# A ninth seven-product pair in a ConvFFN up-projection, next to the step into the down-projection

## The chip, the cores and the metric

The kernel runs on one core of one Trainium2 chip. The metric is the device time of one execution in microseconds, as the median of several runs. The profile is taken from one further execution; its span runs from the first to the last instruction in the trace, and its own device time is given beside it.

## The reference

One layer of a hybrid decoder trunk over 512 tokens of width 1024, all in float32: three causal token mixers whose outputs are gated and merged, then a causal ConvFFN. The change touches only the ConvFFN:

```
def conv_ffn(h, w_up, conv_w, conv_b, w_down):
    up = h @ w_up                      # 512 x 1024 by 1024 x 5632
    padded = jnp.pad(up, ((0, 0), (CONV_WIDTH - 1, 0), (0, 0)))
    conv = conv_b + conv_w[0] * padded[:, 0:T]
    for i in range(1, CONV_WIDTH):
        conv = conv + conv_w[i] * padded[:, i:i + T]
    gate, val = jnp.split(conv, 2, axis=-1)
    return (jax.nn.gelu(gate, approximate=True) * val) @ w_down   # 2816 wide
```

and its result is normalised and added to the residual stream.

## The kernel before, in words

**Precision by splitting.** Every float32 operand of a product is split into a high part (a copy rounded to fp32r, on ACT) and a low part (the rest, a subtraction on DVE). One product of the mathematics is three on TensorE: high by high, high by low, low by high (`mm3`, L111 to L115).

**The up stage.** The 5632 columns are 44 tiles of 128, ordered so that tiles 2n and 2n + 1 make pair n: the gate and the value columns of one block of 128. There are 22 pairs. A plain pair (`up_std`, L1053) takes, for each of its two tiles, eight blocks of the 1024 inputs by three products over all 512 tokens: 48 products of 512 columns. The first two pairs (`FIRST`, L32) were begun in the stage before, for tokens 0 to 255; their other half is written at L1100.

Some pairs go by seven products instead of eight (`up_seven`, L1060, a scheme of the Strassen-Winograd kind). The 2 x 2 block matrix is that of two halves of the inputs by the two tiles of the pair, and the tokens are cut in two halves. Each of the seven block products ("quarters", L1071) is four blocks by three products over 256 tokens, so 12 short products; 84 in all. The weights of the quarters are b11, b21, b22 (blocks as they are) and p1 to p4 (sums of blocks). The sums p3, p2, p1 and p4 are made on GpSimd (L927 to L929 and L948). The token side has four operands ys0 to ys3 that are the same for all patterns: differences of the four blocks of the normalised input, made once by `y_steps` (L854) out of whole blocks (high plus low part, L859), with their own high and low parts (L862, L863). The quarters read b11 and b21 by blocks of the input, then p3 by ys0, p2 by ys1, p1 by ys2, p4 by a block of the input, b22 by ys3.

`SEVEN` (L26) lists the pairs that go so: 5, 7, ..., 19. Each is followed by a plain pair n + 1, the first tile of which is done in pieces between the quarters (L1082 to L1088), so that ACT and DVE can take intermediate results out of PSUM, and the second after the last quarter (L1096). I call the two pairs together a pattern. Pairs 0 to 4 and 21 are plain and stand alone.

**Weights.** `items` (L908) lists the weight pieces in the order of their use; `fill` (L960) splits them ahead into a ring of eight half-tiles, a whole tile taking two, a quarter one. Whole tiles come through two buffers named raw; the blocks of a seven-product pair through the buffers sra and srb, loaded by `s_load` (L919). When b22 of one pattern has been split, the next pattern's blocks are loaded (L952 to L954).

**After each pair,** `up_finish` (L891) does the convolution (ACT L884, DVE L885 and L887), the gelu (L897), the product (L899) and one difference on GpSimd (L902 or L904), into the tile `act`, five slices of eleven blocks. `y_steps` borrows blocks 7 to 10 of three of these slices while they are empty. Pairs 14 and later overwrite them.

**The down stage** is again a seven-product scheme, of seven steps (L983), each with its own weight matrix. These matrices are made by DMA: a buffer of the "chain" is loaded, and for the next step another block is either added into it by an adding DMA that GpSimd issues (L997) or loaded over it by SP (L999). The first step's weights need both: a plain load from SP (L992) and an adding one on top. A chain has six buffers of two blocks (the last of one). `w_prepare` (L1004) splits one and issues the next load into it; `l_prepare` (L1030) splits the left operands, out of `act`, into two tiles. A step takes six chain buffers by two token blocks of 128; one chain buffer is 12 products of 512 columns. Before, chain buffers 0 to 3 lay in the memory of ys0 and ys1 and were loaded after the last pattern (L1111 to L1116), the left operands in that of ys2 and ys3, and chain buffers 4 and 5 in the two raw buffers (L1119 to L1125), while pair 21 ran.

**What sets the order.** The framework that builds the program orders each engine's queue itself, by the place in the program and by a model of when operands are ready: in the trace, the sums of L859 run at 437.6 us, ahead of the convolution of pair 0 at 442.9, though they are written behind it. On the chip each queue then runs strictly in that order, so a queue can stand still at an instruction whose operand is later than modelled.

Of the kernel before, what the change touches and what calls it, by code (L numbers as in the profile page):

```python
# [7 lines left out]
F32 = mybir.dt.float32  # L8
# [14 lines left out]
VC = 656  # L23
NH = NF // 2
TH = T // 2
SEVEN = (5, 7, 9, 11, 13, 15, 17, 19)  # L26
LEVELS = (64, 32, 16, 8, 4, 2, 1)

C_GPRE, C_PSC, C_GN, C_BG, C_CW, C_CB, C_END = 0, 8, 12, 16, 18, 150, 194
# [24 lines left out]
def kernel(ctx: ExitStack, tc: tile.TileContext, x, xT, w_first, w_tiles, w_v, w_br, w_out, w_up, w_down,  # L54
# [776 lines left out]
    with tc.tile_pool(name="fp", bufs=1) as fp:  # L831
# [20 lines left out]
            return tuple(h[:, kh * 4 : kh * 4 + 4, th * TH : (th + 1) * TH] for h in (h2h, h2l))  # L852

        def y_steps():  # L854
            t1, t2, t3 = (act[:, j, 7:11, :] for j in range(3))

            def whole(t, kh, th):
                h, l = hq(kh, th)
                nc.vector.tensor_add(t, h.bitcast(F32), l.bitcast(F32))  # L859

            def parts(i, t):
                nc.scalar.copy(ys[i][:, 0], t)  # L862
                nc.vector.tensor_sub(ys[i][:, 1], t, ys[i][:, 0].bitcast(F32))  # L863

            whole(t1, 0, 1)
            whole(t2, 1, 1)
            nc.vector.tensor_sub(t2, t2, t1)
            yield
            parts(2, t2)
            whole(t3, 0, 0)  # L870
            yield
            nc.vector.tensor_sub(t1, t3, t1)
            parts(0, t1)
            yield
            nc.vector.scalar_tensor_tensor(out=t3, in0=t3, scalar=-1.0, in1=t2, op0=ALU.mult, op1=ALU.subtract)
            parts(1, t3)
            yield
            whole(t1, 1, 0)
            nc.vector.scalar_tensor_tensor(out=t1, in0=t1, scalar=-1.0, in1=t3, op0=ALU.mult, op1=ALU.subtract)
            parts(3, t1)  # L880

        def conv(ps, i):
            t0 = fp.tile([P, T], F32, tag="t0", name="t0", bufs=3)
# [7 lines left out]
        def up_finish(n, pg, pv):  # L891


            i = n // 2
            tg = conv(pg, 2 * n)
            tv = conv(pv, 2 * n + 1)
            nc.scalar.activation(tg, tg, AF.Gelu_apprx_tanh)  # L897
            o = 2 * (n % 2)
            nc.vector.tensor_mul(act[:, o : o + 2, i, :], tg.rearrange("p (h t) -> p h t", h=2),  # L899
                                 tv.rearrange("p (h t) -> p h t", h=2))  # L900
            if n % 2 == 0:
                nc.gpsimd.tensor_sub(act[:, 4, i, :], act[:, 1, i, :], act[:, 0, i, :])  # L902
            else:
                nc.gpsimd.tensor_sub(act[:, 1, i, :], act[:, 1, i, :], act[:, 3, i, :])  # L904
# [14 lines left out]
        def s_load(n):  # L919

            for j, g in enumerate(("sra", "srb")):
                qt[g] = f4(f"{g}{n}", g)
                nc.sync.dma_start(qt[g], w_up[2 * n + j])
            a, b = qt["sra"], qt["srb"]
            for q in ("p1", "p2", "p3"):
                qt[q] = fp.tile([P, T], F32, tag=q, name=f"{q}_{n}")
            nc.gpsimd.tensor_add(qt["p3"], b[:, :T], b[:, T:])  # L927
            nc.gpsimd.tensor_add(qt["p2"], a[:, :T], qt["p3"])
            nc.gpsimd.tensor_add(qt["p1"], a[:, :T], b[:, :T])  # L929
# [7 lines left out]
        def prep(item):  # L937
            if item[0] == "t":
                hi, lo = slots(2)
                raw = load_raw(w_up[item[1]])  # L940
                nc.scalar.copy(hi, raw)  # L941
                nc.vector.tensor_sub(lo, raw, hi.bitcast(F32))  # L942
                return hi, lo
            n, q = item[1:]
            a, b = qt["sra"], qt["srb"]
            if q == "b21":
                r = half(a[:, T:])
                nc.gpsimd.tensor_add(a[:, T:], a[:, T:], qt["p2"])  # L948
                return r
            if q == "b22":  # L950
                r = half(b[:, T:])
                later = [m for m in SEVEN if m > n]  # L952
                if later:
                    s_load(later[0])  # L954
                return r
            return half(a[:, :T] if q == "b11" else a[:, T:] if q == "p4" else qt[q])

# [14 lines left out]
        def up_weight(*item):  # L972
            assert items[done["taken"]] == item, (items[done["taken"]], item)
            done["taken"] += 1
            fill()
            return got_w[item]
# [12 lines left out]
        def chain_load(s, p):  # L989
            k = slice(*pairs[p])  # L990
            if s == 0:
                nc.sync.dma_start(ch[p][:, : (k.stop - k.start) * T].rearrange("p (k c) -> p k c", c=T),  # L992
                                  w_down[0, 1, :, k, :])
            kh, nh = steps[s][1]
            c = ch[p][:, : (k.stop - k.start) * T].rearrange("p (k c) -> p k c", c=T)
            if steps[s][2]:
                nc.gpsimd.dma_start(c, w_down[kh, nh, :, k, :], accum_op=ALU.add)  # L997
            else:
                nc.sync.dma_start(c, w_down[kh, nh, :, k, :])  # L999
# [12 lines left out]
                    chain_load(s + 1, p)  # L1012

        left = {}

        def l_split(s, g):
            k0, k1 = groups[g]
# [17 lines left out]
        def whole_mm(ps, w, kcs):  # L1035
            hi, lo = w
            for kc in kcs:
                c = slice(kc * P, (kc + 1) * P)
                mm3(ps, hi[:, c], lo[:, c], h2h[:, kc, :], h2l[:, kc, :], kc == 0, kc == KC - 1)
# [10 lines left out]
        def yq(i):  # L1050
            return ys[i][:, 0], ys[i][:, 1]
# [8 lines left out]
        def up_seven(n):  # L1060

            bx, by, bz = (psx.tile([P, T], F32, tag="mx", name=f"u{i}_{n}") for i in "xyz")
            pn = [psm.tile([P, T], F32, tag="mm", name=f"up{2 * n + 2 + e}") for e in range(2)]
            ua, ub = (fp.tile([P, T], F32, tag="uo", name=f"u{i}_{n}", bufs=2) for i in "ab")

            def keep(name, ps, scale=1.0):
                t = fp.tile([P, TH], F32, tag="cs", name=name, bufs=4)
                nc.scalar.activation(t, ps[:, :TH], AF.Copy, scale=scale)
                return t

            def quarter(ps, q, y, first):  # L1071
                part_mm(ps, up_weight("s", n, q), y, first)
                free("s", n, q)

            quarter(bx, "b11", hq(0, 0), True)
            q1 = keep("q1", bx)
            quarter(bz, "b21", hq(1, 0), True)
            nc.vector.tensor_add(ua[:, :TH], bz[:, :TH], q1)
            quarter(by, "p3", yq(0), True)
            n7 = keep("n7", by)  # L1080
            w = up_weight("t", 2 * n + 2)
            whole_mm(pn[0], w, range(0, 2))  # L1082
            quarter(bx, "p2", yq(1), False)
            nv = keep("nv", bx)
            whole_mm(pn[0], w, range(2, 5))
            quarter(bx, "p1", yq(2), False)
            u = keep("u", bx, -1.0)
            whole_mm(pn[0], w, range(5, 8))  # L1088
            free("t", 2 * n + 2)
            quarter(by, "p4", hq(1, 1), False)  # L1090
            nc.vector.tensor_add(ua[:, TH:], by[:, :TH], nv)
            nc.vector.tensor_sub(ub[:, TH:], u, n7)
            quarter(bx, "b22", yq(3), False)
            nc.scalar.activation(ub[:, :TH], bx[:, :TH], AF.Copy, scale=-1.0)
            up_finish(n, ua, ub)
            whole_mm(pn[1], up_weight("t", 2 * n + 3), range(KC))  # L1096
            free("t", 2 * n + 3)
            return pn

        for i in range(2 * FIRST):  # L1100
            up_mm(pf[i], up_first[i], slice(256, 512))
        for j in range(FIRST):
            up_finish(j, pf[2 * j], pf[2 * j + 1])
        s_load(SEVEN[0])
        yst = y_steps()
        n = FIRST
        while n < NF:
            if n in SEVEN:
                up_finish(n + 1, *up_seven(n))
                n += 2  # L1110
                if n - 2 == SEVEN[-1]:  # L1111
                    c0 = fp.tile([P, 2, 2 * T], F32, tag="ys0", name="chain01")
                    c1 = fp.tile([P, 2, 2 * T], F32, tag="ys1", name="chain23")
                    ch = [c0[:, 0, :], c0[:, 1, :], c1[:, 0, :], c1[:, 1, :]]
                    for p in range(4):
                        chain_load(0, p)  # L1116
                continue
            pp = up_std(n)
            if n == NF - 1:  # L1119
                lh = [fp.tile([P, 2, 4, TH], F32R, tag=f"ys{i}", name=f"lhs{i}") for i in (2, 3)]  # L1120
                l_prepare(2)
                w_prepare(2)
                ch += [wp.tile([P, 2 * T], F32, tag="raw", name=f"chain{p}", bufs=2) for p in (4, 5)]
                for p in (4, 5):
                    chain_load(0, p)  # L1125
            up_finish(n, *pp)
            for _ in range(3):
                next(yst, None)
            n += 1

# [190 lines left out]
```

## Time and profile before

| what | value |
|---|---|
| median of 3 runs | 774.63 us (774.43 to 775.01) |
| profiled execution, its own time | 774.49 us |
| its span | 772.6 us |
| TensorE busy | 764.5 us, 99% |
| VectorE (DVE) busy | 561.2 us, 73% |
| ScalarE (ACT) busy | 384.4 us, 50% |
| GpSimd (POOL) busy | 128.6 us, 17% |
| up stage, from the second half of pair 0 to the end of pair 21 | 437.8 to 660.9 us |
| down stage, first to last product | 660.9 to 765.8 us |

PE is TensorE's products, PEld its weight loads; SPq and POOLq are the queues from which DMAs are issued. A row of the timeline gives the start, the duration, engine, line and operation, and in brackets the idle time of that engine before it and what ended it. Products overlap in their pipeline, so their rate is read from the distance of their starts, not from their duration. A time "into a pattern" counts from the first product of its first quarter.

### The profile page before, as it was taken

To read this page: it belongs to the slowest core of one execution; us is meant where nothing else is said; L and a number is where in the kernel's file an instruction comes from. 1 tells how busy PE (TensorE), PEld (TensorE's weight loads), DVE (VectorE), ACT (ScalarE), POOL (GpSimd) and SP (SyncE) were. 2 spreads that over 40 slices of the span, in tenths; PEclk is the share of its full clock that TensorE was granted. 3 is DMA by queue.
4 is the path that set the end of the run, shared out by engine and by line. 5 is a ranking of instruction groups with operands and counts; after the bars stand their busy time and mean duration, and the time that the engine had idled before them with its cause. 6 is when DMAs were issued, how large, how long until landed. Compare 5 with 4: busy or idle time off the path is not lost.

```text
span 772.6 us, 10489 instructions
## 1 busy us (share of the span) xinstructions
PE 764.5 (99%) x3974; PEld 647.9 (84%) x3974; DVE 561.2 (73%) x814; ACT 384.4 (50%) x648; POOL 128.6 (17%) x124
## 2 busy tenths in 40 slices
PE   9999999999999999999999999999999999999996
PEld 8899776888887887888888988999989998888885
DVE  5564678378786546555648798888888886887896
ACT  7454654483223433333435374555555556465582
POOL 0100000012404000000000022344333333334000
PEclk9999999999999999999999999999999999999999
DMA  9524121123124212323352131223333329799761
GB/s 328 170 97 137 65 73 67 70 82 108 55 95 137 83 54 82 110 81 109 109 212 88 56 137 55 98 94 110 109 109 109 109 75 269 208 181 189 210 205 54
DMA packets 28529, 92.60 MB, mean 120 GB/s; under 512 B 3392, under 2 KB 3664, under 8 KB 28480
## 3 DMA queue, kind: packets, MB, share of 16 engines
q1 hardware_dynamic: 24048, 77.83, 29.1%
q0 software_dynamic: 4288, 14.11, 9.1%
q8 instruction: 31, 0.51, 0.3%
q14 instruction: 18, 0.15, 0.1%
q10 hardware_dynamic: 144, 0.00, 0.0%
HBM read 89.84 MB, written 2.10 MB: 119 GB/s over the span
## 4 chain that ended last, share of the span: by engine, by line
PE 98%; DVE 0%; DMA 0%; issue 0%; ACT 0%; DVEq 0%
PE pj L113 9%; PE pj L114 9%; PE pj L115 9%; PE up L114 7%; PE up L113 7%; PE up L115 7%; PE ux L1047 6%; PE q L1154 5%; PE q L1156 5%; PE q L1155 5%; PE uy L1047 3%; PE py L115 3%; PE py L114 3%; PE py L113 3%; PE pq L207 3%; PE pz L753 2%
## 5 line engine op out<-in xcount | busy, mean ns | idle before, releaser
L71 ACT CAST whi<-raw 128x1024 fp32r<-128x1024 f32 (+1 forms) x65 | 65.4, 1009 | 135.4 <-PE pj L114 92.6
L113 PE MATMUL pj<-h_hi,whi 128*128 128x512 f32 x296 | 120.9, 408 | 0.0
L114 PE MATMUL pj<-h_lo,whi 128*128 128x512 f32 x296 | 116.1, 392 | 0.0
L115 PE MATMUL pj<-h_hi,wlo 128*128 128x512 f32 x296 | 115.8, 391 | 0.0
L72 DVE TENSOR_TENSOR wlo<-raw,whi 128x1024 fp32r<-128x1024 f32 (+1 forms) x65 | 76.3, 1178 | 51.2 <-ACT whi L71 51.1
L113 PE MATMUL up<-h_hi,whi 128*128 128x512 f32 (+1 forms) x256 | 94.3, 370 | 0.0
L114 PE MATMUL up<-h_lo,whi 128*128 128x512 f32 (+1 forms) x256 | 93.4, 365 | 0.0
L115 PE MATMUL up<-h_hi,wlo 128*128 128x512 f32 (+1 forms) x256 | 92.7, 362 | 0.0
L113 PEld LDWEIGHTS pj<-h_hi,whi 128*128 128x128 f32 x296 | 55.7, 188 | 16.2 <-issue 3.7
L115 PEld LDWEIGHTS pj<-h_hi,wlo 128*128 128x128 f32 x296 | 55.6, 188 | 12.0 <-issue 0.2
L114 PEld LDWEIGHTS pj<-h_lo,whi 128*128 128x128 f32 x296 | 55.8, 188 | 10.7 <-issue 1.2
L1154 PE MATMUL q<-whi,lhs 128*128 128x512 f32 x154 | 59.9, 389 | 0.0
L1155 PE MATMUL q<-wlo,lhs 128*128 128x512 f32 x154 | 59.9, 389 | 0.0
L1156 PE MATMUL q<-whi,lhs 128*128 128x512 f32 x154 | 59.9, 389 | 0.0
L72 DVE TENSOR_TENSOR wlo<-chain,whi 128x1024 fp32r<-128x1024 f32 (+1 forms) x42 | 49.1, 1181 | 8.9 <-ACT whi L71 8.9
L115 PEld LDWEIGHTS up<-h_hi,wlo 128*128 128x128 f32 x256 | 48.3, 189 | 7.8
L113 PEld LDWEIGHTS up<-h_hi,whi 128*128 128x128 f32 x256 | 48.2, 189 | 6.6
L114 PEld LDWEIGHTS up<-h_lo,whi 128*128 128x128 f32 x256 | 48.4, 189 | 6.3
L71 ACT CAST whi<-chain 128x1024 fp32r<-128x1024 f32 (+1 forms) x42 | 41.0, 978 | 24.0 <-PE q L1156 19.1
L927 POOL TENSOR_TENSOR p<-srb 128x512 f32<-128x512 f32 x8 | 10.8, 1354 | 217.7 <-DMA srb<-in_w_up_dram 217.7
L676 DVE TENSOR_TENSOR g<-pj,rstd_b 128x512 f32<-128x512 f32 x24 | 16.4, 687 | 27.3 <-PE pj L115 27.3
L942 DVE TENSOR_TENSOR wlo<-raw,whi 128x1024 fp32r<-128x1024 f32 x24 | 33.7, 1403 | 3.1 <-ACT whi L941 3.0
(351 smaller groups left out, 1777.4 us busy)
## 6 DMA issues: line engine op xcount, KB each, us to landing
raw<-in_w_tiles_dram SPq DMA_DIRECT2D x37, 512.0 KB, 3.3
raw<-in_w_up_dram SPq DMA_DIRECT2D x28, 512.0 KB, 3.4
chain<-in_w_down_dram SPq DMA_DIRECT2D x20, 512.0 KB, 4.7
chain<-in_w_down_dram POOLq DMA_DIRECT2D x20, 512.0 KB, 7.5
raw<-in_w_br_dram SPq DMA_DIRECT2D x12, 512.0 KB, 3.3
raw<-in_w_out_dram SPq DMA_DIRECT2D x8, 512.0 KB, 3.3
sra<-in_w_up_dram SPq DMA_DIRECT2D x8, 512.0 KB, 3.1
srb<-in_w_up_dram SPq DMA_DIRECT2D x8, 512.0 KB, 3.3
```

Of the source, the lines that this page charges most:

```text
L71: nc.scalar.copy(hi[:, c], raw[:, c])
L72: nc.vector.tensor_sub(lo[:, c], raw[:, c], hi[:, c].bitcast(F32))
L113: nc.tensor.matmul(ps, lh, rh, start=first, stop=False)
L114: nc.tensor.matmul(ps, lh, rl, start=False, stop=False)
L115: nc.tensor.matmul(ps, ll, rh, start=False, stop=last)
L207: nc.tensor.matmul(pq[i], w[:, kc, i * P : (i + 1) * P], h[:, kc, :], start=kc == 0 and n == 0, stop=kc == KC - 1 and n == 2)
L676: nc.vector.tensor_mul(g1, gates.pop((br, m)), rstd_b)
L942: nc.vector.tensor_sub(lo, raw, hi.bitcast(F32))
L1047: nc.tensor.matmul(ps[:, :TH], x[:, c], y[:, kc, :], start=first and kc == 0 and t == 0, stop=kc == 3 and t == 2, skip_group_check=not first)
L1154: nc.tensor.matmul(ps, hi, wh[:, c], start=k == 0 and not last, stop=False, skip_group_check=last)
L1155: nc.tensor.matmul(ps, hi, wl[:, c], start=False, stop=False, skip_group_check=last)
L1156: nc.tensor.matmul(ps, lo, wh[:, c], start=False, stop=k == NH - 1, skip_group_check=last)
```

## The change

1. `SEVEN` becomes 4, 6, ..., 20. The pairs that stand alone are 0 to 3; the ninth pattern takes pairs 20 and 21, so the up stage ends with a pattern.
2. The four whole blocks for `y_steps` are summed on GpSimd at once, into four slices of `act`, and written ahead of the products of pairs 0 and 1, behind `s_load` of the first pattern, which moves there too. The rest of `y_steps` is spread over the finishes of pairs 1, 2 and 3, and its order is ys0, ys1, ys2, ys3.
3. The chain's first buffers lie elsewhere: 0 and 1 in sra and srb, loaded as soon as b22 of the last pattern has been split; 2 and 3 in ys0, loaded after the quarter p3; 4 and 5 in the raw buffers as before. Splitting of the first left operands and the first two chain buffers and the loads of 4 and 5 are written inside the last pattern, behind its last quarter and ahead of its last plain tile.

```diff
-SEVEN = (5, 7, 9, 11, 13, 15, 17, 19)
+SEVEN = (4, 6, 8, 10, 12, 14, 16, 18, 20)
...
         def y_steps():
-            t1, t2, t3 = (act[:, j, 7:11, :] for j in range(3))
-
-            def whole(t, kh, th):
+
+            whole = [act[:, j, 7:11, :] for j in range(4)]
+            t1, t2, t3, t4 = whole
+            for t, (kh, th) in zip((t3, t1, t2, t4), ((0, 0), (0, 1), (1, 1), (1, 0))):
                 h, l = hq(kh, th)
-                nc.vector.tensor_add(t, h.bitcast(F32), l.bitcast(F32))
+                nc.gpsimd.tensor_add(t, h.bitcast(F32), l.bitcast(F32))
...
-            whole(t1, 0, 1)
-            whole(t2, 1, 1)
+            yield
             nc.vector.tensor_sub(t2, t2, t1)
-            yield
-            parts(2, t2)
-            whole(t3, 0, 0)
-            yield
             nc.vector.tensor_sub(t1, t3, t1)
             parts(0, t1)
             yield
             nc.vector.scalar_tensor_tensor(out=t3, in0=t3, scalar=-1.0, in1=t2, op0=ALU.mult, op1=ALU.subtract)
             parts(1, t3)
             yield
-            whole(t1, 1, 0)
-            nc.vector.scalar_tensor_tensor(out=t1, in0=t1, scalar=-1.0, in1=t3, op0=ALU.mult, op1=ALU.subtract)
-            parts(3, t1)
+            parts(2, t2)
+            yield
+            nc.vector.scalar_tensor_tensor(out=t4, in0=t4, scalar=-1.0, in1=t3, op0=ALU.mult, op1=ALU.subtract)
+            parts(3, t4)
...
                 later = [m for m in SEVEN if m > n]
                 if later:
                     s_load(later[0])
+                else:
+                    ch[:2] = [f4(f"chain{j}", g) for j, g in enumerate(("sra", "srb"))]
+                    for p in range(2):
+                        chain_load(0, p)
...
             quarter(by, "p3", yq(0), True)
+            if n == SEVEN[-1]:
+                c1 = fp.tile([P, 2, 2 * T], F32, tag="ys0", name="chain23")
+                ch[2:4] = [c1[:, 0, :], c1[:, 1, :]]
+                for p in (2, 3):
+                    chain_load(0, p)
...
             up_finish(n, ua, ub)
+            if n == SEVEN[-1]:
+                lh[:] = [fp.tile([P, 2, 4, TH], F32R, tag=f"ys{i}", name=f"lhs{i}") for i in (2, 3)]
+                l_prepare(2)
+                w_prepare(2)
+                ch[4:] = [wp.tile([P, 2 * T], F32, tag="raw", name=f"chain{p}", bufs=2) for p in (4, 5)]
+                for p in (4, 5):
+                    chain_load(0, p)
             whole_mm(pn[1], up_weight("t", 2 * n + 3), range(KC))
...
+        s_load(SEVEN[0])
+        yst = y_steps()
+        next(yst)
         for i in range(2 * FIRST):
             up_mm(pf[i], up_first[i], slice(256, 512))
         for j in range(FIRST):
             up_finish(j, pf[2 * j], pf[2 * j + 1])
-        s_load(SEVEN[0])
-        yst = y_steps()
+            if j:
+                next(yst)
...
                 up_finish(n + 1, *up_seven(n))
                 n += 2
-                if n - 2 == SEVEN[-1]:
-                    c0 = fp.tile([P, 2, 2 * T], F32, tag="ys0", name="chain01")
-                    c1 = fp.tile([P, 2, 2 * T], F32, tag="ys1", name="chain23")
-                    ch = [c0[:, 0, :], c0[:, 1, :], c1[:, 0, :], c1[:, 1, :]]
-                    for p in range(4):
-                        chain_load(0, p)
                 continue
             pp = up_std(n)
-            if n == NF - 1:
-                lh = [fp.tile([P, 2, 4, TH], F32R, tag=f"ys{i}", name=f"lhs{i}") for i in (2, 3)]
-                l_prepare(2)
-                w_prepare(2)
-                ch += [wp.tile([P, 2 * T], F32, tag="raw", name=f"chain{p}", bufs=2) for p in (4, 5)]
-                for p in (4, 5):
-                    chain_load(0, p)
             up_finish(n, *pp)
-            for _ in range(3):
+            for _ in range(2):
                 next(yst, None)
             n += 1
```

More of the change, by code (lines that the diff above doesn't have):

```diff
@@ L1014 @@
         left = {}
+        lh, ch = [], []
         def l_split(s, g):
```

## Prediction

> **What bounds the kernel now.** I read the page's head first, then the waits of TensorE, then the busy times by stage.
>
> ```profile
> span 772.6 us, 10489 instructions
> PE 764.5 (99%) x3974; PEld 647.9 (84%) x3974; DVE 561.2 (73%) x814; ACT 384.4 (50%) x648; POOL 128.6 (17%) x124
> ...
> PE   9999999999999999999999999999999999999996
> ...
> PE 98%; DVE 0%; DMA 0%; issue 0%; ACT 0%; DVEq 0%
> ```
>
> ```profile
> PE warm L183 <- POOL ones L167: 1.0, 1, 1.0
> PE pq L207 <- DVE w_hi L193: 0.2, 1, 0.2
> ```
>
> TensorE is on the chain for 98% of the span, and the second answer holds every wait of it in the whole run: 1.2 us, all at the very start. In the up stage and at the step into the down stage it waits for nothing. So two things alone can move the time: the number of TensorE cycles between the first product and the last, and a wait that is new. By stage:
>
> ```profile
> 449.07:459.95 10.88, 10.88 (x50) 9.02 (x49) 10.88 (x14) 6.41 (x8) 2.33 (x2) 1.00 0.43 145
> 459.95:470.83 10.88, 10.88 (x49) 9.01 (x48) 10.88 (x14) 6.08 (x9) 4.55 (x2) 1.00 0.27 98
> 470.83:481.70 10.87, 10.87 (x49) 9.01 (x48) 8.12 (x10) 5.05 (x7) 0.80 (x2) 1.00 0.14 48
> 481.70:502.74 21.04, 21.04 (x133) 19.08 (x133) 16.73 (x20) 11.24 (x19) 6.74 (x5) 1.00 0.28 99
> 607.97:629.01 21.04, 21.04 (x133) 19.08 (x132) 17.96 (x23) 11.81 (x21) 7.85 (x6) 1.00 0.30 100
> 629.01:650.06 21.05, 21.05 (x134) 19.08 (x133) 13.45 (x19) 11.35 (x18) 5.37 (x6) 1.00 0.75 207
> 650.06:660.94 10.88, 10.88 (x50) 9.02 (x49) 10.74 (x14) 5.86 (x8) 4.14 (x4) 1.00 1.07 258
> ```
>
> The columns are length, busy time (instructions) of PE, PEld, DVE, ACT and POOL, granted clock, DMA share, GB/s. The rows are, in order, plain pairs 2, 3 and 4, the patterns that begin at pairs 5, 17 and 19 (each a seven-product pair with a plain one in it), and plain pair 21. Every row is solid TensorE at clock 1.00. A plain pair is 10.88 us, a pattern 21.04.
>
> **What TensorE saves.** The change turns four plain pairs and eight patterns into two plain pairs and nine patterns: before 4 x 10.88 + 8 x 21.04 = 211.84 us, after 2 x 10.88 + 9 x 21.04 = 211.12. That is 0.72 us less. The gain is small although an eighth of the multiplications goes, and the rows say why:
>
> ```profile
> 481.90 1.43 PE ux L1047 x12
> 483.33 1.44 PE uz L1047 x12
> ```
>
> Twelve products of 256 columns take 1.44 us, 0.120 each. A plain pair is 48 products of 512 columns in 10.88, 0.2267 each, so half of one would be 0.1133. The seven-product pair issues 84 short ones, 84 x 0.120 = 10.08, against 10.88: 0.80 us saved, not 10.88/8 = 1.36; the other 0.08 goes where a pattern changes between lengths. The Trainium skill (TensorE: Matmul & The Clock Gate, Back-to-back issue gap) gives the isolated gap as N/2.4 + 2.5 ns; by it the pair would be 84 x 109.2 = 9.17 us against 48 x 215.8 = 10.36, an estimate of 1.19 us saved and a run at about 773.3. The trace has 120 and 226.7 ns in this kernel, so I take 0.72.
>
> **The start: row sums on GpSimd.** The loads of the first pattern are written ahead of the products of pairs 0 and 1, but they already ran as early as they can: behind the last transposes of the stage before, whose memory they take.
>
> ```profile
> 437.71 0.33 SPq L923 DMA_DIRECT2D sra<-in_w_up_dram  x1
> ...
> 442.35 1.77 POOL L927 TENSOR_TENSOR p<-srb 128x512 f32<-128x512 f32 x1 [198.25 <-DMA srb<-in_w_up_dram]
> 444.09 2.27 POOL L929 TENSOR_TENSOR p<-sra,srb 128x512 f32<-128x512 f32 x1
> 446.32 1.29 POOL L928 TENSOR_TENSOR p<-sra,p 128x512 f32<-128x512 f32 x1
> ```
>
> ```profile
> 439.36 2.35 DVE L859 TENSOR_TENSOR act<-h_hi,h_lo 128x1024 f32<-128x1024 f32 x2
> ...
> 443.54 1.67 DVE L942 TENSOR_TENSOR wlo<-raw,whi 128x1024 fp32r<-128x1024 f32 x1
> ...
> 446.45 2.25 DVE L942 TENSOR_TENSOR wlo<-raw,whi 128x1024 fp32r<-128x1024 f32 x1
> ...
> 451.68 1.31 DVE L942 TENSOR_TENSOR wlo<-raw,whi 128x1024 fp32r<-128x1024 f32 x1
> 452.92 0.73 DVE L887 SCALAR_TENSOR_TENSOR t<-up,small_sb,t 128x510 f32<-128x510 f32 x1
> ```
>
> On SP's queue nothing is passed: the next loads there are those of pair 2, before and after. DVE is rid of four sums of 1.2 us, 4.8 in all. GpSimd gets them. No row has one of 1024 elements on GpSimd; its sums of 512 take 1.29 to 2.27, so one of 1024 lies between 2.58 and 4.54, four between 10.3 and 18.2. I take some 3, since DVE is emptier at that time. At the worst, all four behind the three sums that end at 447.61, they end at 465.8. From there the first row operand needs two sums on DVE, a copy on ACT (1.05) and a subtraction, 4.65 us, and is there at 470.4. The quarter that reads it is the third of a pattern, 2 x 1.44 = 2.88 us in, now at 470.83 + 2.88 = 473.71. The other three operands take 3.45, 2.25 and 3.45 us of work more each, for quarters that start after three, four and six quarters with 6, 15 and 24 long products between them: 5.7, 9.2 and 14.1 us in. All are in time, so I cost this at nothing. Its cover is TensorE's two plain pairs. If the cover fails, it is by DVE's queue (the second rival).
>
> The price shows elsewhere: while GpSimd sums, DVE's subtractions take 1.67 and 2.25 us instead of 1.2 to 1.3. DVE was busy for all of 449.07 to 470.83. With one pattern begun a plain pair sooner it has two weight tiles (2.4 us) and four sums (4.8) less to do by then; at most some eight DVE operations can meet those ten us of GpSimd, each 0.4 to 1.0 us longer, which gives back 3 to 8. It about evens out.
>
> **The end: the last pattern runs into the down stage.** Before, pair 21's 10.88 us lay between the last pattern and the first down product. Now the last pattern starts at 470.83 + 8 x 21.04 = 639.15 and the first down product is due at 660.19 (660.94 before). The first weights of the down stage take a plain load, an adding load by GpSimd on top, a copy on ACT, a subtraction on DVE:
>
> ```profile
> 633.52 0.80 SPq L992 DMA_DIRECT2D chain<-in_w_down_dram  x2
> ...
> 638.00 1.89 POOL L997 DMA_DIRECT2D chain<-in_w_down_dram  x2 [2.89 <-DMA chain<-in_w_down_dram]
> ...
> 646.96 1.05 ACT L71 CAST whi<-chain 128x1024 fp32r<-128x1024 f32 x1 [3.00 <-DMA chain<-in_w_down_dram]
> ...
> 648.04 1.22 DVE L72 TENSOR_TENSOR wlo<-chain,whi 128x1024 fp32r<-128x1024 f32 x1 [2.12 <-ACT whi L71]
> ...
> 655.54 2.04 DVE L72 TENSOR_TENSOR wlo<-chain,whi 128x1024 fp32r<-128x1024 f32 x1
> ```
>
> That is 13.44 us from load to landing and 2.30 more to the end of the split. These loads now take the buffers sra and srb, which come free where the next pattern's loads started before:
>
> ```profile
> 611.30 0.33 SPq L923 DMA_DIRECT2D sra<-in_w_up_dram  x1
> 613.49 0.33 SPq L923 DMA_DIRECT2D srb<-in_w_up_dram  x1
> ```
>
> These are 3.33 and 5.52 us after 607.97. So chain 0 is loaded from 642.48, lands at 655.92 and is split at 658.22, 2.0 us before TensorE asks for it. Chain 1 starts at 644.67; its products come 12 x 0.2267 = 2.72 later, at 662.91. For it the answers on the chain tile give the landings of plain loads (first row, issues at 633 to 637) and of the adding ones with a plain load beside them (second, 637 to 640):
>
> ```profile
> DMA to landing us min/median/max: 3.9/4.8/6.2
> ```
>
> ```profile
> DMA to landing us min/median/max: 6.2/8.7/11.5
> ```
>
> By the medians chain 1 lands 13.5 us after its load, at 658.2, and is split at 660.5, 2.4 early; by the longest (17.7) it is split at 664.7, 1.8 late. Chain 0 by the longest is split at 662.5, 2.3 late. With 0.82 us for a split beside a busy GpSimd (2.04 against 1.22) the worst is 3.1. The best is no wait. Chains 2 and 3 start at 643.5, when the quarter before has read its operand, and are due 5.4 and 8.2 us after 660.19, so they are easier, and 4 and 5, due 10.9 and 13.6 us in, easier still. I take no wait, since the copy that waited for chain 0 in the trace gives the nearest row. The Trainium skill (DMA: Bandwidth & Descriptors, Anatomy of one DMA) fits a transfer issued by GpSimd as 2.0 us + bytes/436e3; for 512 KB that is an estimate of 3.2 us and would leave over 5 us to spare and the sum at 773.8. The trace has 6.2 to 11.5 for an adding load, so it doesn't decide it; the trace leaves the margin thin.
>
> New in the queues: ACT's copy of chain 0 now may wait until 655.9, and behind it stand the last activation of the pattern's output, the convolutions of pairs 20 and 21 and the second left operand. The latter is due 5.4 us into the stage; the PSUM banks behind the former are wanted a step (15 us) later. That is their cover.
>
> **Sum.** 774.49 - 0.72 + 0 = 773.77 for the profiled execution; the span would be 771.9, and 1.89 us lie around it. The median of the runs, 774.63, is 0.14 above that execution; I give 773.8. A difference of 0.2% is 1.55 us, about what a measurement of this kernel can tell from none, so the forecast is no change.
>
> **Rivals.** First, the handover waits: chain 0 or 1 lands late, TensorE stands still before its first down products. It begins to cost when an adding load lands over 2 us later than the 13.44 of the trace, and it is slower than before by over 0.2% from a wait of 2.27 us. For it: the time from the first load to the first product shrinks from 27.4 to 17.7 us, and the stretch 650.06:660.94 had DMA share 1.07, so they fight for the same engines. Against: four of six are issued within 2.2 us, when plain loads were fastest. A worst wait of 3.1 gives 774.49 - 0.72 + 3.1 = 776.9; a mild one of 1 gives 774.8.
>
> Second, DVE blocked at the start: a sum of the row operands stands in its queue before GpSimd is done. With sums of 4.54 the third ends at 447.61 + 13.6 = 461.2; behind it stand the split of pair 3's weights (451.68 above) and the convolution that gives back a PSUM bank (452.92), both due at 459.95. Two DVE sums, that split and that step are 4.4 us, done at 465.6: a wait of 5.7 us, 779.5. It decides only if the queue's order puts the sum ahead of both and GpSimd is at its slowest; at 3 us per sum the third ends at 456.6 and nothing waits. The Trainium skill (GPSIMD Engine Reference, Engine selection) speaks against this part: it calls two-input elementwise work on GpSimd about half as fast as on VectorE. The trace agrees (1.29 or more for 512 elements, where DVE took 1.18 for 1024), and at that rate the cover holds.
>
> Third, a larger gain: were short products half the price of long ones, the ninth seven-product pair would save 1.36 us: 774.49 - 1.36 = 773.1. The rows of 0.120 us are against it, and even it stays within 0.2%.
>
> **Chances.** No wait, 0.54. Handover wait under 2.27 us, 0.19; over it, 0.13. Blocked DVE at the start, 0.06. Larger gain, 0.04, of which none is over 0.2%; for something I don't see, 0.04, half faster and half slower by more than the bound. So faster 0.02, same 0.77, slower 0.21. The range runs from the larger of the gains and the spread of the runs (774.63 - 0.8 - 0.3, the distance of the lowest and highest run from the median being 0.2 and 0.4: some 773.5) to a handover wait of 2.6 us (776.4); what lies above has about 0.16, below 0.03. The likeliest case alone is 773.5 to 774.3.
>
> **What would show it.** Nine pattern rows of 21.04 us, the first at 470.8; no TensorE wait in the up stage; chain 0's copy at about 656 after a DMA wait, first down product at 660.2; four GpSimd sums of 1024 elements of 2.6 to 4.5 us before 466. A line in TensorE's waits on ACT or DVE for the chain's weights, or a gap before 660 to 663, proves the first rival; one between 455 and 472 the second. Patterns that are longer than 21.04 would break the sum itself.

## The result and the profile after

The changed kernel takes 787.34 us (786.98 to 788.19, 4 runs), the kernel before 774.82 beside it: 12.5 us slower, a ratio of 1.0165 (95% interval 1.0152 to 1.0178). The prediction was no change, 773.8, with a range from 773.5 to 776.4. It was wrong.

The page's first lines and the waits of TensorE (in all, times, longest), after:

```profile
span 785.2 us, 10596 instructions
PE 768.6 (98%) x4010; PEld 651.4 (83%) x4010; DVE 558.6 (71%) x818; ACT 386.8 (49%) x658; POOL 147.1 (19%) x132
```

```profile
PE up L113 <- DVE t L884: 4.7, 1, 4.7
PE q L1159 <- DVE wlo L72: 3.1, 2, 2.7
...
PE q L1158 <- ACT whi L71: 0.9, 1, 0.9
```

TensorE, which waited for nothing after its start, now waits once at the start of the up stage, for the convolution on DVE that gives a PSUM bank back, and three times for weights of the down stage. The busy times by stretch (length, busy time of PE, PEld, DVE, ACT, POOL, then the granted clock):

```profile
449.00:454.00 5.00, 0.27 (x2) 0.23 (x2) 5.00 (x5) 3.24 (x4) 5.00 (x3) 0.83 0.30 105
454.00:459.00 5.00, 5.00 (x12) 3.91 (x13) 5.00 (x7) 4.66 (x7) 0.87 (x2) 0.50 0.30 105
459.00:464.00 5.00, 5.00 (x23) 4.05 (x22) 5.00 (x8) 3.20 (x5) 0.00 (x0) 0.99 0.45 148
...
646.52:667.56 21.04, 21.04 (x134) 19.07 (x132) 10.17 (x15) 7.32 (x12) 8.17 (x8) 1.00 0.91 231
...
678.00:681.00 3.00, 3.00 (x7) 2.42 (x8) 3.00 (x4) 1.90 (x3) 3.00 (x2) 0.50 0.61 173
```

The last pattern is 21.04 us long, as forecast, but its first product starts at 646.52, not at 639.15: 7.37 us are lost before it. A wait of 4.73 is the larger part. The rest, 2.64, fits the clock, which stood at half for the first 5.3 us of work after the wait: the row of 454 to 459 counts 12 products, that of the next 5 us 23. From the first down product (667.56) to the end of the span it is 117.64 us, against 772.6 - 660.94 = 111.66 before: 5.98 lost. Of this 4.01 are the listed waits and 1.5 the clock, at half for 3.0 us of work (677.97 to 681). The remaining 0.5 fits the restarts: a listed wait is counted from the modelled end of the product before, 0.39 us after its start, while products otherwise start 0.227 apart, so each wait costs some 0.16 us more than it says. With the 0.72 saved: 7.37 + 5.98 - 0.72 = 12.63, and the spans differ by 12.6.

**The start**, on GpSimd, DVE and TensorE:

```profile
438.02 9.47 POOL L860 TENSOR_TENSOR act<-h_hi,h_lo 128x1024 f32<-128x1024 f32 x4 [194.04 <-PE pz L803]
```

```profile
438.11 0.69 DVE L807 TENSOR_TENSOR h_lo<-pz,h_hi 128x512 fp32r<-128x512 f32 x1 [1.18 <-ACT h_hi L806]
445.16 3.41 DVE L867 TENSOR_TENSOR act<-act 128x1024 f32<-128x1024 f32 x1 [6.36 <-POOL act L860]
448.49 2.30 DVE L939 TENSOR_TENSOR wlo<-raw,whi 128x1024 fp32r<-128x1024 f32 x1
450.72 0.74 DVE L882 SCALAR_TENSOR_TENSOR t<-up,small_sb,t 128x511 f32<-128x511 f32 x1
451.38 1.62 DVE L868 TENSOR_TENSOR act<-act 128x1024 f32<-128x1024 f32 x1
452.92 0.73 DVE L884 SCALAR_TENSOR_TENSOR t<-up,small_sb,t 128x510 f32<-128x510 f32 x1
```

```profile
453.81 0.77 PE L113 MATMUL up<-h_hi,whi 128*128 128x512 f32 x1 [4.73 <-DVE t L884]
```

The four sums took 9.47 us together, 2.4 each, below the lowest price that I gave them. But DVE's first row step (L867) stands in its queue ahead of everything of the up stage, and waits until 445.16 for the third of them: DVE is idle for 6.36 us. That step then runs beside the fourth sum and takes 3.41 us instead of 1.2, the next subtraction 2.30. Only then comes the convolution of pair 0 (450.72 and 452.92), which was done at 445.9 before, and TensorE waits for its bank.

**The end**, on ACT, DVE and TensorE:

```profile
657.63 1.04 ACT L1026 CAST lhs<-act 128x1024 fp32r<-128x1024 f32 x1
663.42 1.05 ACT L71 CAST whi<-chain 128x1024 fp32r<-128x1024 f32 x1 [4.74 <-DMA chain<-in_w_down_dram]
668.66 1.05 ACT L71 CAST whi<-chain 128x1024 fp32r<-128x1024 f32 x1 [4.19 <-DMA chain<-in_w_down_dram]
669.61 0.81 ACT L881 ACTIVATE t<-ua,small_sb 128x512 f32<-128x512 f32 x1
...
673.65 1.98 ACT L71 CAST whi<-chain 128x1024 fp32r<-128x1024 f32 x2
```

```profile
669.74 1.23 DVE L72 TENSOR_TENSOR wlo<-chain,whi 128x1024 fp32r<-128x1024 f32 x1 [3.68 <-ACT whi L71]
...
672.33 1.22 DVE L1027 TENSOR_TENSOR lhs<-act,lhs 128x1024 fp32r<-128x1024 f32 x1
...
676.70 1.22 DVE L72 TENSOR_TENSOR wlo<-chain,whi 128x1024 fp32r<-128x1024 f32 x1
```

```profile
671.02 0.50 PE L1159 MATMUL q<-wlo,lhs 128*128 128x512 f32 x1 [0.35 <-DVE wlo L72]
674.73 0.50 PE L1158 MATMUL q<-whi,lhs 128*128 128x512 f32 x1 [0.92 <-ACT whi L71]
677.97 0.79 PE L1159 MATMUL q<-wlo,lhs 128*128 128x512 f32 x1 [2.74 <-DVE wlo L72]
```

Chain 0's copy starts at its landing, 663.42 - 646.52 = 16.90 us into the last pattern; the prediction had 16.77. Chain 1's starts at 668.66, 22.1 in, and costs TensorE 0.35 us. But ACT stands still at these two copies for 8.9 us, and DVE behind ACT, with the convolutions of pairs 20 and 21 and the second left operand queued behind. All of that is done from 669.6 on, ahead of chain 2, whose split ends only at 677.9. The large waits, 0.92 and 2.74, are for chain 2: for its copy (the first of the two at 673.65) and for the subtraction behind it (676.70).

Chain 2 itself was not late. Its adding load and the time that this load took to land:

```profile
657.14 0.86 POOL L998 DMA_DIRECT2D chain<-in_w_down_dram  x1 [0.39 <-issue]
```

```profile
DMA to landing us min/median/max: 9.0/9.0/9.0
```

It landed at 657.14 + 9.0 = 666.1, some 2.5 us before chain 1, and lay there until ACT came to it at 673.65.

### The profile page after: what moved, and what is told of

Read it like the earlier page. It is cut to its first block, busy times and chain, and to the rows that moved or that the text cites. A ratio compares the mean times of both kernels' runs of the same rounds, so it can differ in the third digit from the quotient of the medians.

```text
span 785.2 us, 10596 instructions
## 1 busy us (share of the span) xinstructions
PE 768.6 (98%) x4010; PEld 651.4 (83%) x4010; DVE 558.6 (71%) x818; ACT 386.8 (49%) x658; POOL 147.1 (19%) x132
## 4 chain that ended last, share of the span: by engine, by line
PE 94%; DVE 2%; DMA 2%; POOL 1%; issue 1%; ACT 0%; DVEq 0%; POOLq 0%; ACTq 0%
PE pj L113 9%; PE pj L114 9%; PE pj L115 9%; PE ux L1049 6%; PE up L113 5%; PE up L114 5%; PE up L115 5%; PE q L1159 4%; PE q L1160 4%; PE q L1158 4%; PE uy L1049 3%; PE py L115 3%; PE py L113 3%; PE py L114 3%; PE pq L207 3%; PE pz L751 2%
## 5 line engine op out<-in xcount | busy, mean ns | idle before, releaser
L113 PE MATMUL up<-h_hi,whi 128*128 128x512 f32 (+1 forms) x240 | 89.4, 373 | 4.7 <-DVE t L884 4.7
L114 PE MATMUL up<-h_lo,whi 128*128 128x512 f32 (+1 forms) x240 | 88.2, 368 | 0.0
L115 PE MATMUL up<-h_hi,wlo 128*128 128x512 f32 (+1 forms) x240 | 87.4, 365 | 0.0
L113 PEld LDWEIGHTS up<-h_hi,whi 128*128 128x128 f32 x240 | 46.0, 192 | 11.0 <-issue 4.9
L115 PEld LDWEIGHTS up<-h_hi,wlo 128*128 128x128 f32 x240 | 45.8, 191 | 7.4
L114 PEld LDWEIGHTS up<-h_lo,whi 128*128 128x128 f32 x240 | 46.0, 192 | 5.8
L860 POOL TENSOR_TENSOR act<-h_hi,h_lo 128x1024 f32<-128x1024 f32 x4 | 9.5, 2400 | 194.0 <-PE pz L803 194.0
L1049 PE MATMUL ux<-ys,whi 128*128 128x256 f32 x216 | 39.9, 283 | 0.0
L1159 PEld LDWEIGHTS q<-wlo,lhs 128*128 128x128 f32 x154 | 29.3, 190 | 9.9 <-DVE wlo L72 3.8
```

Of the source, the lines that this page charges most:

```text
L113: nc.tensor.matmul(ps, lh, rh, start=first, stop=False)
L114: nc.tensor.matmul(ps, lh, rl, start=False, stop=False)
L115: nc.tensor.matmul(ps, ll, rh, start=False, stop=last)
L860: nc.gpsimd.tensor_add(t, h.bitcast(F32), l.bitcast(F32))
L1049: nc.tensor.matmul(ps[:, :TH], x[:, c], y[:, kc, :], start=first and kc == 0 and t == 0, stop=kc == 3 and t == 2, skip_group_check=not first)
L1159: nc.tensor.matmul(ps, hi, wl[:, c], start=False, stop=False, skip_group_check=last)
```

## The experiments

My theory after the traces: two separate losses, each an instruction that stands in an in-order queue ahead of work that is due sooner, each made dearer by the clock. The rivals: one is a consequence of the other; GpSimd's sums slow DVE whatever the order; the landings alone make the loss at the end; DVE has too much to do there anyhow.

**e1_first8, the new start alone.**

```diff
-SEVEN = (4, 6, 8, 10, 12, 14, 16, 18, 20)
+SEVEN = (4, 6, 8, 10, 12, 14, 16, 18)
...
```

The chain's loads, `l_prepare` and `w_prepare` stand where they stood before the change.

> The new start alone: patterns at pairs 4 to 18, pairs 20 and 21 plain, the step into the down stage as before. TensorE's work is that of before. Theory (two separate losses; at the start DVE's first row step stands in its queue until GpSimd has summed, 4.7 us of wait and 2.8 us of lowered clock): 774.8 + 7.5 = 782.3, with a wait of about 4.7 us ahead of pair 2 and none at the down stage. Rival (what is late at the end comes from the start or from GpSimd's share): a loss beyond that, at the down stage too, 785 or more.

781.07 us against 774.56, 6.5 more. Its only wait behind the very first products:

```profile
PE up L113 <- DVE t L884: 4.7, 1, 4.7
```

No wait at the down stage, so the start does not cause the end. The clock cost less than in the changed kernel, as told in the part on the prediction.

**e2_last8, the new end alone.**

```diff
-SEVEN = (5, 7, 9, 11, 13, 15, 17, 19)
+SEVEN = (6, 8, 10, 12, 14, 16, 18, 20)
...
```

`y_steps` and its place are those before the change, the chain's buffers and loads those of the change.

> The new end alone: patterns at pairs 6 to 20, pairs 0 to 5 plain, the row sums on DVE as before. Theory (the down stage's first weights come late by themselves): three waits of 4.0 us in all at the first down products and 1.8 us of lowered clock, 774.8 + 5.8 = 780.6. Rival (the end is late only behind the new start): no wait, 774.8.

781.30 us, 6.7 more, with the same three waits. The first of the rivals falls: 6.5 + 6.7 - 0.7 = 12.5, the whole loss, from two parts that do not need each other. That the sum comes out to 0.1 us is partly luck: the time at half clock after the waits was 2.9 us in e1 and 5.6 in e2, against 5.3 and 3.0 in the changed kernel.

```profile
664.25 0.50 PE L1159 MATMUL q<-wlo,lhs 128*128 128x512 f32 x1 [0.49 <-DVE wlo L72]
...
667.96 0.50 PE L1158 MATMUL q<-whi,lhs 128*128 128x512 f32 x1 [0.93 <-ACT whi L71]
671.20 0.80 PE L1159 MATMUL q<-wlo,lhs 128*128 128x512 f32 x1 [2.74 <-DVE wlo L72]
```

**e3_dvesums.**

```diff
-                nc.gpsimd.tensor_add(t, h.bitcast(F32), l.bitcast(F32))
+                nc.vector.tensor_add(t, h.bitcast(F32), l.bitcast(F32))
```

> The whole change with the four row sums on DVE. Theory: the wait at the start goes, the end keeps its 5.8 us: 774.8 - 0.7 + 5.8 = 779.9. Rival (the start is slow because the sums are begun ahead of the first convolutions, on whichever engine): a wait ahead of pair 2 remains, 782 or more.

781.13 us. The wait of 4.73 and its half clock are gone; 0.72 remains, for the split of pair 2's weights, so four sums begun at once are a little too much for DVE too. That is 1.2 more than expected: this wait, and a wait for chain 1 of 0.70 in place of 0.35.

**e4_held, GpSimd's sums kept, the order in DVE's queue changed.**

```diff
+            if n == 0:
+                nc.vector.tensor_scalar(one, tv[:, 4:5], 0.0, 1.0, op0=ALU.mult, op1=ALU.add)
...
-            nc.vector.tensor_sub(t2, t2, t1)
+            nc.vector.scalar_tensor_tensor(out=t2, in0=t2, scalar=one, in1=t1, op0=ALU.mult, op1=ALU.subtract)
```

> The whole change with the sums on GpSimd as they are, but DVE's first row step made to wait for the convolution of pair 0 (it multiplies by a 1 that is computed from that). Theory (only the order in DVE's queue): as with the sums on DVE, 779.9, no wait ahead of pair 2. Rival (GpSimd's sums slow DVE's subtractions, whatever the order): a wait of 2 us or more ahead of pairs 2 or 3, 782 to 785.

783.13 us, and no wait ahead of pairs 2 or 3: with the same sums on the same engine, the order alone takes the 4.73 us away. By the medians the kernel is slower than e3 by 2.0. Its profile shows two other waits in the first pattern, 0.33 and this one:

```profile
487.29 0.51 PE L1053 MATMUL ux<-ys,whi 128*128 128x256 f32 x2 [1.56 <-ACT u L1074]
```

```profile
485.03 1.27 POOL L928 TENSOR_TENSOR p<-srb 128x512 f32<-128x512 f32 x1 [4.71 <-DMA srb<-in_w_up_dram]
```

```profile
486.34 0.62 ACT L934 CAST whi<-p 128x512 fp32r<-128x512 f32 x1 [3.40 <-POOL p L928]
486.86 0.38 ACT L1074 ACTIVATE u<-ux 128x256 f32<-128x256 f32 x1
```

Here ACT stands at a copy of the next pattern's weights, which waits for a sum on GpSimd, and behind it is the activation that TensorE needs. It is the same kind of loss at a third place. GpSimd was not busy with row sums then (they ended at 449.6): its sum had itself waited 4.71 us for the load of the next pattern's blocks, which was issued 10.0 us into the first pattern, against 6.0 in e3. Whether DVE's longer operations beside GpSimd made that load late I did not try apart; the rival is weakened, not excluded. Nor do the 2.0 us belong to this wait for certain: the two profiled executions have the same span, 780.0, and e4's (781.81) was the fastest of its four.

**e5_oldstart, nine patterns with the row operands made as before the change.**

```diff
-            for t, (kh, th) in zip((t3, t1, t2, t4), ((0, 0), (0, 1), (1, 1), (1, 0))):
-                h, l = hq(kh, th)
-                nc.gpsimd.tensor_add(t, h.bitcast(F32), l.bitcast(F32))
+            def whole(t, kh, th):
+                h, l = hq(kh, th)
+                nc.vector.tensor_add(t, h.bitcast(F32), l.bitcast(F32))
...
-            for _ in range(2):
+            for _ in range(3):
                 next(yst, None)
```

> Nine patterns and the change's end, with the row operands made as before: sums on DVE, one step at a time behind the finishes. Theory (the start costs nothing with that order, the end is its own loss): no wait before 660 us, waits of 4 us at the first down products, 774.6 - 0.7 + 6.2 = 780.1. Rival (two plain pairs are too short a cover for the row operands on DVE): a wait at the first pattern, 782 or more.

780.22 us. No wait before 666 us: two plain pairs are cover enough for the old row sums. The ones begun sooner on GpSimd bought nothing. Two waits remain:

```profile
PE q L1159 <- DVE wlo L72: 2.7, 1, 2.7
...
PE q L1158 <- ACT whi L71: 0.9, 1, 0.9
```

Both are for chain 2; for chain 1 no wait is listed. So the 3.7 us come even when chain 1 is in time for TensorE.

**e6_noadd, e5 without the adding loads of the first down step.**

```diff
+            if s == 0:
+                return
             if steps[s][2]:
                 nc.gpsimd.dma_start(c, w_down[kh, nh, :, k, :], accum_op=ALU.add)
```

> As e5, without the six adding loads of the down stage's first step, so that its weights are the plain blocks and not the sums. Theory (the late landing starts the loss at the end): the weights land some 8 us sooner, no wait, 774.6 - 0.7 = 773.9. Rival (ACT and DVE have too much to do between the last quarter and the first down products, landing or not): waits of 2 us or more remain, 777 to 780.

773.86 us (10 runs; 774.59 before), ratio 0.9990 (0.9981 to 0.9999), no wait behind the start. This kernel leaves out six additions and so computes something else; it is a probe. ACT and DVE have the same work at the handover as in e5, so it is not too much: the late landing starts the loss.

**e7_hold, e5 with four copies of ACT held back.**

```diff
+            if n == SEVEN[-1]:
+                nc.vector.tensor_scalar(one, tg[:, 4:5], 0.0, 1.0, op0=ALU.mult, op1=ALU.add)
...
-                split(ch[p], hi, lo, slice(0, (k1 - k0) * T))
+                if s == 0 and p in (0, 1, 2, 3):
+                    nc.scalar.activation(hi[:, : (k1 - k0) * T], ch[p][:, : (k1 - k0) * T], AF.Copy, scale=one)
+                    nc.vector.tensor_sub(lo[:, : (k1 - k0) * T], ch[p][:, : (k1 - k0) * T], hi[:, : (k1 - k0) * T].bitcast(F32))
+                else:
+                    split(ch[p], hi, lo, slice(0, (k1 - k0) * T))
```

> As e5, with the copies of the first four chain buffers on ACT made to wait for the first convolution of pair 20, so that they stand behind the left operands and that convolution in ACT's queue; the loads are as before. Theory (chain 1 itself is only some 0.4 us late; the queues that stand still behind its copy make 4 us of it): waits under 1 us in all, 774 to 775.5. Rival (the landings alone make the loss): waits of 3 us or more, 779 to 781.

775.41 us, ratio 1.0007 (0.9998 to 1.0016), with the loads where they were. Two waits remain, longer together than I had expected, and neither lowers the clock:

```profile
664.22 0.50 PE L1167 MATMUL q<-wlo,lhs 128*128 128x512 f32 x1 [0.69 <-DVE wlo L1019]
```

```profile
668.04 0.50 PE L1167 MATMUL q<-wlo,lhs 128*128 128x512 f32 x1 [0.80 <-DVE wlo L1019]
```

The first is for chain 1, whose copy waits for its landing (661.75). The second is for chain 2 and again one of order: its copy was done by 663.94, but DVE's subtraction for it stands behind a convolution, which waits for an activation on ACT, which stands behind the copy of chain 3 and its landing.

```profile
661.75 2.19 ACT L1018 ACTIVATE whi<-chain,one 128x1024 fp32r<-128x1024 f32 x2 [2.47 <-DMA chain<-in_w_down_dram]
664.25 1.15 ACT L1018 ACTIVATE whi<-chain,one 128x1024 fp32r<-128x1024 f32 x1 [0.31 <-DMA chain<-in_w_down_dram]
```

```profile
666.10 0.75 DVE L887 SCALAR_TENSOR_TENSOR t<-up,small_sb,t 128x511 f32<-128x511 f32 x1 [1.28 <-ACT t L886]
666.77 1.22 DVE L1019 TENSOR_TENSOR wlo<-chain,whi 128x1024 fp32r<-128x1024 f32 x1
```

So of the 6.4 us that e5 loses against e6, 4.8 go with this one change of the order in ACT's queue (the half clock included). Of the 1.6 that stay, about half is chain 1's landing; the rest still depends on the order.

**e8_swap, e7 and the chain's buffers permuted.** Chain 4's buffer is filled first: it is the raw buffer of an earlier tile. Now it holds chain 0.

```diff
+                    ch[:] = [None] + [f4(f"chain{j + 1}", g) for j, g in enumerate(("sra", "srb"))] + [None] * 3
...
+                ch[3:5] = [c1[:, 0, :], c1[:, 1, :]]
...
             w = up_weight("t", 2 * n + 2)
+            if n == SEVEN[-1]:
+                for p in (0, 5):
+                    ch[p] = wp.tile([P, 2 * T], F32, tag="raw", name=f"chain{p}", bufs=2)
+                    chain_load(0, p)
```

The copies held back are now those of 1 to 4.

> As e7, and the chain's buffers change places: the raw buffer that comes free earliest holds chain 0, sra and srb hold 1 and 2, ys0 3 and 4, the other raw buffer 5. Theory (every landing is then some 3 us or more ahead of its use): no wait at the down stage and 773.9, 0.7 less than the kernel before. Rival (what DVE has to do at the handover is the bound once the landings are not): waits of 1 us or more, 775.5 or above.

773.85 us (11 runs), ratio 0.9989 (0.9981 to 0.9998): as fast as e6, with all additions in, and 0.74 below the kernel before. The waits of TensorE in it, and its last pattern with the stretch that follows:

```profile
PE warm L183 <- POOL ones L167: 1.0, 1, 1.0
PE pq L207 <- DVE w_hi L193: 0.7, 1, 0.7
```

```profile
639.00:660.04 21.04, 21.04 (x133) 19.08 (x132) 14.98 (x23) 12.41 (x19) 8.16 (x8) 1.00 0.90 239
660.04:676.00 15.96, 15.96 (x72) 13.23 (x71) 14.42 (x16) 10.88 (x13) 8.65 (x6) 1.00 0.76 244
```

TensorE is solid from pattern into down stage, within 0.2 us of the times that the prediction gave for the change (pattern at 639.15, down stage at 660.19).

## Why the prediction was wrong

**The saving was right.** 0.72 us were forecast from the stage table, the last pattern is 21.04 us long, and the two kernels without a wait, e6 and e8, are 0.73 and 0.74 below the kernel before. These ratios alone are loose, with intervals that reach from 0.1 to 1.5 us. The traces say it closer: from the first product of the up stage to the end of the last of the down stage it is 423.98 to 765.82 before, 341.84 us, and 423.80 to 764.92 in e8, 341.12.

**"I cost this at nothing. Its cover is TensorE's two plain pairs"** failed. I asked when the row operands would be ready (in time) and who needs them, and not what stands behind the first DVE step that waits for GpSimd. The second rival had that mechanism, at 0.06, with the sum in front of pair 1's convolution and GpSimd at its slowest. It was in front of pair 0's, due 11 us sooner, and so it cost 4.73 us with GpSimd at its fastest. That rival was also worked out too kindly: at 3 us per sum its own 4.4 us of DVE work end at 456.6 + 4.4 = 461.0, behind the 459.95 at which they are due, and not with nothing waiting. The row that should have told me was one that I described in the text ahead of the prediction: the sums ran at 437.6, in front of the convolution at 442.9, although written behind it. So the first row step would be placed there too, wherever the change wrote it.

**"That is their cover"** failed at the end. The landing of chain 0 was right to 0.13 us, and chain 1 was late by 0.35 us, within the bounds. "I take no wait" was wrong all the same, by 4.01 us. But the first rival priced the wait by the lateness of one landing, at most 3.1 us, and I let what was queued behind the copies be covered by when its own results were due. The missing term is the work held up on ACT and DVE, which comes before chain 2's split although chain 2 had landed; e7 shows that 4.8 us hang on that order.

**The clock was no term of the sum.** Some 2.6 and 1.5 us of the 12.6 came from it. Rows of single microseconds of the changed kernel:

```profile
452.00:453.00 1.00, 0.00 (x0) 0.00 (x0) 1.00 (x2) 0.00 (x0) 1.00 (x1) 0.65 0.95 340
453.00:454.00 1.00, 0.20 (x1) 0.23 (x2) 1.00 (x2) 0.97 (x1) 1.00 (x1) 0.50 0.32 127
459.00:460.00 1.00, 1.00 (x5) 0.79 (x4) 1.00 (x2) 1.00 (x2) 0.00 (x0) 0.94 0.00 0
```

TensorE stands from 449.1 to 453.8; the granted clock falls to half at 452.3 (0.65 over that microsecond is 0.3 at full clock and 0.7 at half), and is back only at 459.1, 5.3 us into work. In e1 the same wait brought half of that cost: there the clock fell at 453.5 and came back at 456.9, 2.9 us into work:

```profile
453.00:454.00 1.00, 0.00 (x0) 0.00 (x0) 1.00 (x3) 0.68 (x1) 1.00 (x1) 0.76 0.69 274
456.00:457.00 1.00, 1.00 (x4) 0.81 (x3) 1.00 (x2) 1.00 (x3) 0.00 (x0) 0.53 0.19 57
```

The waits of 0.92 and 2.74 close together did it too. In e5 it fell at 668.5, 0.8 us into the second of them, when TensorE had stood for 1.7 of the 3.4 us before:

```profile
668.00:669.00 1.00, 0.00 (x0) 0.00 (x0) 1.00 (x2) 0.34 (x2) 0.00 (x0) 0.74 0.01 4
```

The single wait of 1.56 in e4 (485.7 to 487.3) and those of 0.69 and 0.80 in e7 did not:

```profile
488.00:490.00 2.00, 2.00 (x15) 1.78 (x14) 2.00 (x3) 0.00 (x0) 1.23 (x1) 1.00 0.00 0
```

The Trainium skill (TensorE: Matmul & The Clock Gate, Part 1) has a rule for it: a clock gate that watches windows of about 3.4 us which run freely, halves the clock after an idle one and releases it after a busy one. The runs agree with the half and with the windows: every stretch at half clock behind a wait lasted one or two times 3.4 us, 6.8 here (452.3 to 459.1), in e2 and in e5, and 3.4 in e1, e3, e4 and at the end of the changed kernel (677.6 to 681.0). So the same wait costs one window or two, by where it falls. They do not agree that the window must be idle as a whole: in e5 it was idle for half. By that rule a wait of 4.7 us should have been priced at up to 3.4 us more, two windows at half clock (an estimate from the skill's 3.4 us); the runs had 1.4 (e1) to 2.8 (e2).

**The larger gain** (the third rival) did not come, as the rows of 0.120 us said.

What stays open: why three of e4's four executions took 783.0 us or more, when the fourth, the profiled one, took 781.81; and whether GpSimd's sums lengthened DVE's work enough in e4 to bring about its wait on ACT.

## What to carry to other kernels

Before moving a producer to a slower engine, find the consumer's place in its own queue and price everything behind it until the producer ends: being ready in time is not enough, since a queue in order passes the delay to whatever is due soonest. Where a framework orders the queues by a model, look in the trace for instructions that ran ahead of their place in the program; they tell where the next one will be put. On a kernel that TensorE bounds, a saving of under 1 us is only worth taking with the waits at zero, because a wait can bring a half clock with it (here one of 4.7 us, and two of 0.9 and 2.7 close together); the same ninth pattern was 12.5 us slower or 0.7 faster by the order of the row sums and a few copies and the choice of a buffer.

## What the runs showed of the hardware

Four row sums of 1024 elements on GpSimd took 9.47 us when DVE was idle beside most of them (2.37 each, less than twice the cheapest sum of 512, 1.29) and 11.46 when it worked beside most of them (e4). DVE's own operations on two operands of 1024 elements in SBUF took 1.6 to 3.4 us instead of 1.2 while GpSimd summed, and its convolutions out of PSUM stayed at 0.73 to 0.75:

```profile
438.17 11.46 POOL L862 TENSOR_TENSOR act<-h_hi,h_lo 128x1024 f32<-128x1024 f32 x4 [194.01 <-PE pz L803]
```
